# Four edits to a two-layer, four-way attention kernel: a scan operand, a one-column multiply, half of a subtraction and a scaling step change their place

## The chip, the cores and the metric

The kernel runs on one core of one Trainium2 chip. A core has TensorE (PE in the profile, its weight loads PEld), VectorE (DVE), ScalarE (ACT), GpSimd (POOL) and a queue engine (SP) that issues the transfers; they share the on-chip memory SBUF, and TensorE writes into PSUM, where this kernel has eight tiles of 128 partitions by 512 float32. The metric is the device time of one execution in microseconds (us), as the median of some runs.

## The reference

Two layers over a sequence of 2048 tokens, width 1024. Each layer projects the tokens, runs four groups of four heads (head size 64), gates, projects back and normalises:

- fox: causal softmax attention with a forget term; mla: causal softmax attention with low-rank projections and rotary parts; mem: softmax attention over 256 memory rows;
- sb, "stick-breaking": with z the scaled logits, the weight of key k for query q is `sigmoid(z[q,k])` times the product of `sigmoid(-z[q,k'])` over all valid keys k' behind k (k < k' < q). In the reference this product is the exponential of a reverse cumulative sum of `log_sigmoid(-z)`.

```
z = einsum('bhqd,bhkd->bhqk', qb, k) * scale
log_keep = where(valid, log_sigmoid(-z), 0)
log_tail = cumsum(log_keep, reverse) - log_keep
w = where(valid, exp(log_sigmoid(z) + log_tail), 0)
```

All is float32; the kernel carries each matrix operand as a float16 high part and a float16 low part.

## The kernel before, in words

Each layer goes through a list of stages (PLAN): the latent projections, then two head pairs each of fox, mla, sb and mem, then the output projection with its layer norm. A pair's work runs in four chunks of 512 queries: project keys, queries and values and the gate, then for each of the two heads and for each group g of two query tiles (128 queries each, j = 0 and 1; tile i = 2g + j) the attention. Keys are taken in blocks b of up to 1024: query tile i has one block of (i+1)*128 columns, or for i of 8 and more two blocks, (i-7)*128 and 1024 columns.

What happens to one sb block (`stick_tile`, `half`): PE writes the scores of up to 512 keys each into PSUM tiles `ps` (one or two a block, out of four buffers that scores and gates share). ACT makes two sigmoids of each `ps` into SBUF, `keep` (L400) and `w` (L401). DVE runs a product scan backwards over `keep` in place (L403): its first input is `keep`, its second operand is not used (op1 is bypass) and is `keep` again; it starts from `cy`, which is a constant for the last keys and for the other block the running product, copied out by L408. POOL multiplies the last column of `w` by `cy` (L404) and the other columns of `w` by the scanned `keep`, shifted by one (L405). ACT casts `w` to float16 (`hi`, L411), DVE subtracts that from `w` to the float16 low half (`lo`, L412), and SP issues the transposing transfer of both halves (L354), whose result PE multiplies with the values (L859). The tiles `hi`/`lo` have three buffers.

What happens to the softmax kinds (`softmax_tiles`, fox and mla): DVE copies the scores from PSUM to SBUF with a row maximum (L369 with the forget term, L371 without), reduces the maxima of both query tiles (L376) and scales them (L377, one instruction of 128x2); ACT takes the exponentials in place (L381), casts to `hi` (L388), POOL subtracts to `lo` (L389).

Each engine works through its own queue in order. The order of the queues is not written by hand: a planner lays the instructions out along its own estimate of the timeline, by the order in the program and by what is ready, so that instructions of neighbouring blocks and of the next chunk's projections stand between those of one block.

Of the kernel before, what the change touches and what calls it, by code (L numbers as in the profile page):

```python
# [13 lines left out]
AF = mybir.ActivationFunctionType  # L14
ALU = mybir.AluOpType
# [6 lines left out]
P = 128  # L22
# [18 lines left out]
LN_TOP = 15.0 * math.log(2.0)  # L41
# [8 lines left out]
def hybrid_kernel(ctx: ExitStack, tc: tile.TileContext, x, mem, ln_in_g, ln_in_b, mem_ln_g, mem_ln_b,  # L50
# [7 lines left out]
    def pool(name, bufs, space=None):  # L58
        if space is None:
            return ctx.enter_context(tc.tile_pool(name=name, bufs=bufs))  # L60
        return ctx.enter_context(tc.tile_pool(name=name, bufs=bufs, space=space))
# [13 lines left out]
    op = pool("op", 1)  # L75
# [8 lines left out]
    V, A, G, T = nc.vector, nc.scalar, nc.gpsimd, nc.tensor  # L84
# [4 lines left out]
    def nm(s):  # L89
        uid[0] += 1  # L90
        return f"{s}_{uid[0]}"
# [135 lines left out]
    def granule(name, shape=(P, 1024), dt=F32):  # L227
        return sbp.tile(list(shape), dt, name=nm(name), tag="sb")
# [89 lines left out]
    def scores(kind, h, i, b, qs, ks, qr, kr):  # L318

        n = min(1024, (i + 1) * P - 1024 * b)  # L320
        j = i % 4
        npass = 3 if kind == "mla" else 2
        parts = []
        with tc.high_priority(offset=SCORE_AHEAD.get(kind, 0)):
            for o in range(0, n, 512):
                c, m = 2 * b + o // 512, min(512, n - o)
                ps = s_tile()
                diag = c == i // 4
                for v in range(npass):
                    last = v == npass - 1 and not diag  # L330
                    if v < 2:
                        T.matmul(ps[:, :m], qs[:, h, v, j * P:(j + 1) * P], ks[c][:, h, :m], start=(v == 0), stop=last)  # L332
                    else:
                        T.matmul(ps[:, :m], qr[:, h, j * P:(j + 1) * P], kr[:, c * 4:c * 4 + m // P, :], start=False, stop=last)
                if diag:
                    T.matmul(ps[:, m - P:m], id_bf, masks["s" if kind == "sb" else "c"], start=False, stop=True)
                parts.append((ps, o, m))
        return parts, n
# [9 lines left out]
    def hl_tile(n):  # L348

        t = phl.tile([P, 2048], F16, name=nm("hl"), tag="phl")  # L350
        return t[:, :n], t[:, n:2 * n], t[:, :2 * n]

    def emit_T(both, n, pt, j):
        dmaT(pt[:, 16 * j:16 * j + 2 * (n // P), :], both)  # L354

    def softmax_tiles(kind, h, g, qs, ks, qr, kr, fb, sc, nsc, su):

        sm = smp.tile([P, 2, 8], F32, name=nm("sm"), tag="sm", bufs=8)
        nb = g // 4 + 1
        at, n_ = [[], []], [0, 0]  # L360
        for j in range(2):
            for b in range(nb):
                parts, n = scores(kind, h, 2 * g + j, b, qs, ks, qr, kr)
                t = granule("sb")[:, :n]
                for ps, o, m in parts:
                    mx = sm[:, j, 4 + n_[j]:5 + n_[j]]
                    n_[j] += 1
                    if kind == "fox":
                        V.tensor_tensor_reduce(t[:, o:o + m], ps[:, :m], fb[b][:, o:o + m], 1.0, -3.0e38, ALU.add, ALU.max, mx)  # L369
                    else:  # L370
                        V.tensor_scalar(t[:, o:o + m], ps[:, :m], 1.0, None, op0=ALU.mult, op1=ALU.max, accum_out=mx)  # L371
                at[j].append(t)
        top = sm[:, :, 4:5]
        if n_[0] > 1:
            top = sm[:, :, 0:1]
            V.tensor_reduce(top, sm[:, :, 4:4 + n_[0]], axis=AX.X, op=ALU.max)  # L376
        V.tensor_scalar(sm[:, :, 2:3], top, nsc, LN_TOP, op0=ALU.mult, op1=ALU.add)  # L377
        col = h * 4 + 2 * (g % 2)
        for j in range(2):
            for b, t in enumerate(at[j]):  # L380
                A.activation(t, t, AF.Exp, scale=sc, bias=sm[:, j, 2:3], accum_out=su[:, b, col + j:col + j + 1])  # L381

        def half(b, pt):
            for j in range(2):
                t = at[j][b]
                n = min(1024, (2 * g + j + 1) * P - 1024 * b)
                hi, lo, both = hl_tile(n)
                A.copy(hi, t)  # L388
                G.tensor_tensor(lo, t, hi, op=ALU.subtract)  # L389
                emit_T(both, n, pt, j)  # L390
        return half

    def stick_tile(h, i, j, qs, ks, sc, nsc):
        carry = [None]

        def half(b, pt):
            parts, n = scores("sb", h, i, b, qs, ks, None, None)
            keep, w = granule("kp")[:, :n], granule("sg")[:, :n]
            for ps, o, m in parts:
                A.activation(keep[:, o:o + m], ps[:, :m], AF.Sigmoid, scale=nsc)  # L400
                A.activation(w[:, o:o + m], ps[:, :m], AF.Sigmoid, scale=sc)  # L401
            cy = TOP if carry[0] is None else carry[0]
            V.tensor_tensor_scan(keep[:, ::-1], keep[:, ::-1], keep[:, ::-1], cy, op0=ALU.mult, op1=ALU.bypass)  # L403
            G.tensor_scalar(w[:, n - 1:n], w[:, n - 1:n], cy, 1.0, op0=ALU.mult, op1=ALU.mult)  # L404
            G.tensor_tensor(w[:, :n - 1], w[:, :n - 1], keep[:, 1:n], op=ALU.mult)  # L405
            if b:
                ct = smp.tile([P, 8], F32, name=nm("cy"), tag="cy", bufs=8)
                V.tensor_copy(ct[:, 0:1], keep[:, 0:1])  # L408
                carry[0] = ct[:, 0:1]
            hi, lo, both = hl_tile(n)  # L410
            A.copy(hi, w)  # L411
            V.tensor_tensor(lo, w, hi, op=ALU.subtract)  # L412
            emit_T(both, n, pt, j)
        return half

# [49 lines left out]
    def layer(l, hT, s_h, u_h, ah):  # L465
# [241 lines left out]
        def pair(kind, p):  # L707
# [54 lines left out]
            for c in range(NCH):  # L762
# [32 lines left out]
                for h in range(2):  # L795
# [34 lines left out]
                    for g in (2 * c, 2 * c + 1):  # L830
                        nb = (2 * g + 1) // 8 + 1
                        halves = []
                        if kind == "sb":
                            for j in range(2):
                                halves.append(stick_tile(h, 2 * g + j, j, qs, ks, sc, nsc))
                        else:
                            halves.append(softmax_tiles(kind, h, g, qs, ks, qr, kr, fb, sc, nsc, su))
# [235 lines left out]
```

## Time and profile before

| | |
|---|---|
| median of 3 runs | 3155.57 us (3152.43 to 3160.11) |
| the profiled execution's own time | 3160.48 us |
| its span | 3158.5 us |
| PE busy | 2557.1 us (81%) |
| DVE busy | 2280.7 us (72%) |
| ACT busy | 1913.3 us (61%) |
| POOL busy | 1561.7 us (49%) |
| mean granted TensorE clock | 0.91 |

The span runs from the first to the last instruction. Busy time is the time in which an engine has at least one instruction running; an instruction that has begun and is held up inside counts as busy. Matmuls overlap, so PE's busy time is more than what its array needs. The profile gives a chain of work that ended last, groups of instructions by source line, what ended each idle time, a timeline, and sums over any stretch. The two sb stages of layer 0 lie at some 870 to 1300 us, those of layer 1 at some 2400 to 2840 us; the fox and mla stages lie ahead of them, from some 250 and 1770 us.

### The profile page before, as it was taken

How to read it: one execution, taken by the hardware profiler on the slowest of the kernel's cores; microseconds unless marked ns; L12 is line 12 of the kernel's file. 1: busy time of each engine (PE TensorE's matmuls, PEld its weight loads, DVE VectorE, ACT ScalarE, POOL GpSimd, SP SyncE). 2: the span in 40 equal slices, each digit the busy share in tenths (PEclk: the TensorE clock that was granted, in tenths of full speed). 3: DMA queues.
4: the chain of work that ended last, by engine and by line, in shares of the span. 5: the costliest groups of instructions: out<-in, count | busy, mean ns of one | idle time of the engine just before them, and what ended most of it. 6: DMA issues, size and time to landing. Idle time of an engine off the chain costs nothing. (4 is left out here: it accounts for less than half of the span.)

```text
span 3158.5 us, 47091 instructions
## 1 busy us (share of the span) xinstructions
PE 2557.1 (81%) x16412; PEld 1374.9 (44%) x16412; DVE 2280.7 (72%) x4377; ACT 1913.3 (61%) x3543; POOL 1561.7 (49%) x1079
## 2 busy tenths in 40 slices
PE   2589897888986784798978899878889768659898
PEld 2345453444553442444434545444445435334443
DVE  7756767867679989757655475577676998994565
ACT  3447667877766676474234566677767766755600
POOL 5305545555678687443210246455657867772400
PEclk9889998999998897799989999999989889769999
DMA  7748978888755745657845478897977475465752
GB/s 190 196 126 167 191 154 188 176 174 174 150 103 115 155 87 112 139 119 191 235 116 126 90 162 163 165 189 157 176 157 135 91 168 101 96 148 114 170 181 100
DMA packets 1225038, 469.46 MB, mean 149 GB/s; under 512 B 1040304, under 2 KB 1184944, under 8 KB 1224656
## 3 DMA queue, kind: packets, MB, share of 16 engines
q1 hardware_dynamic: 1224800, 466.46, 67.8%
q8 instruction: 128, 2.10, 0.3%
q14 instruction: 110, 0.90, 0.1%
HBM read 141.07 MB, written 50.53 MB: 61 GB/s over the span
## 5 line engine op out<-in xcount | busy, mean ns | idle before, releaser
L389 POOL TENSOR_TENSOR hl<-sb,hl 128x1024 f16<-128x1024 f32 (+7 forms) x384 | 609.1, 1599 | 686.3 <-ACT hl L388 503.9
L332 PE MATMUL s<-k,q 128*128 128x512 f16 (+3 forms) x1920 | 529.4, 378 | 117.7 <-ACT sg L401 34.0
L859 PE MATMUL o<-pt,v 128*128 128x256 f16 (+3 forms) x3456 | 429.4, 299 | 200.3 <-DMA pt<-hl 194.8
L405 POOL TENSOR_TENSOR sg<-sg,kp 128x127 f32<-128x127 f32 (+3 forms) x192 | 384.4, 2004 | 119.7 <-DVE kp L403 95.3
L381 ACT ACTIVATE sb<-sb,sm,sc_all 128x1024 f32<-128x1024 f32 (+7 forms) x384 | 376.5, 981 | 76.0 <-DVE sm L377 75.4
L859 PEld LDWEIGHTS <-v 128*64 128x64 f16 (+1 forms) x3456 | 245.0, 112 | 401.7 <-DMA pt<-hl 201.3
L388 ACT CAST hl<-sb 128x1024 f16<-128x1024 f32 (+7 forms) x384 | 297.7, 791 | 184.2 <-DMA pt<-hl 174.0
L937 PE MATMUL s<-wo,gc 128*128 128x512 f16 x1536 | 335.2, 381 | 0.4 <-DVE yt L941 0.4
L332 PEld LDWEIGHTS <-q 128*128 128x128 f16 x1920 | 185.2, 104 | 321.0 <-issue 201.8
L412 DVE TENSOR_TENSOR hl<-sg,hl 128x128 f16<-128x128 f32 (+3 forms) x192 | 241.9, 1267 | 44.0 <-ACT hl L411 43.0
L411 ACT CAST hl<-sg 128x128 f16<-128x128 f32 (+3 forms) x192 | 152.9, 798 | 177.5 <-DMA pt<-hl 104.4
L369 DVE CUSTOM_DVE_ANT_0 sb<-s,fb 128x512 f32<-128x512 f32 (+2 forms) x320 | 184.3, 607 | 102.9 <-DMA fb<-fds 39.6
L371 DVE TENSOR_SCALAR_CACHE_REDUCE sb<-s 128x512 f32<-128x512 f32 (+2 forms) x320 | 185.5, 606 | 72.1 <-POOL hl L389 39.8
L937 PEld LDWEIGHTS <-gc 128*128 128x128 f16 x1536 | 150.9, 98 | 182.2 <-issue 3.9
L401 ACT ACTIVATE sg<-s,sc_all 128x512 f32<-128x512 f32 (+2 forms) x320 | 199.6, 629 | 40.4 <-POOL sg L405 22.1
L403 DVE TENSOR_TENSOR_SCAN kp<-kp 128x384 f32<-128x384 f32 (+7 forms) x128 | 216.6, 1705 | 8.8 <-ACT kp L400 7.7
L400 ACT ACTIVATE kp<-s,sc_all 128x512 f32<-128x512 f32 (+2 forms) x320 | 200.0, 627 | 29.0 <-PE s L332 9.4
L276 PE MATMUL pv<-w,hT 128*128 128x128 f16 x1024 | 191.6, 227 | 24.6 <-DVE k L286 24.6
L456 POOL TENSOR_TENSOR og<-og,sg 128x512 f32<-128x512 f32 x64 | 99.2, 1550 | 223.2 <-DVE og L452 124.0
L276 PE MATMUL pg<-hT,w 128*128 128x512 f16 x512 | 197.0, 385 | 8.1 <-DVE sb L371 3.7
L277 PE MATMUL pg<-hT,w 128*128 128x512 f16 x512 | 196.3, 383 | 0.0
L278 PE MATMUL pg<-hT,w 128*128 128x512 f16 x512 | 195.9, 383 | 0.0
(238 smaller groups left out, 5930.1 us busy)
## 6 DMA issues: line engine op xcount, KB each, us to landing
raw<-in_w_in_dram SPq DMA_DIRECT2D x100, 256.0 KB, 4.7
q<-q SPq DMA_DIRECT2D x128, 128.0 KB, 2.8
fb<-fds SPq DMA_DIRECT2D x32, 512.0 KB, 4.0
gd<-gh SPq DMA_DIRECT2D x128, 128.0 KB, 2.6
raw<-in_w_out_dram SPq DMA_DIRECT2D x64, 256.0 KB, 3.8
gc<-gd SPq DMA_DIRECT2D x64, 256.0 KB, 4.0
yt<-ah SPq DMA_DIRECT2D x32, 512.0 KB, 5.3
raw<-ctd SPq DMA_DIRECT2D x48, 256.0 KB, 3.1
```

The costliest lines, as they stand in the source:

```text
L276: T.matmul(ps, lh, rh, start=(first and k == 0), stop=False)
L332: T.matmul(ps[:, :m], qs[:, h, v, j * P:(j + 1) * P], ks[c][:, h, :m], start=(v == 0), stop=last)
L381: A.activation(t, t, AF.Exp, scale=sc, bias=sm[:, j, 2:3], accum_out=su[:, b, col + j:col + j + 1])
L388: A.copy(hi, t)
L389: G.tensor_tensor(lo, t, hi, op=ALU.subtract)
L400: A.activation(keep[:, o:o + m], ps[:, :m], AF.Sigmoid, scale=nsc)
L401: A.activation(w[:, o:o + m], ps[:, :m], AF.Sigmoid, scale=sc)
L403: V.tensor_tensor_scan(keep[:, ::-1], keep[:, ::-1], keep[:, ::-1], cy, op0=ALU.mult, op1=ALU.bypass)
L405: G.tensor_tensor(w[:, :n - 1], w[:, :n - 1], keep[:, 1:n], op=ALU.mult)
L412: V.tensor_tensor(lo, w, hi, op=ALU.subtract)
L859: T.matmul(o[r0:r1, oc + j0 * P:oc + 256], vs[k // 4][:, k % 4, h, 0:r1 - r0], pcol(pt, a, k % 8, kb, j0), start=(n == 1), stop=(n == total))
L937: T.matmul(ps, gc[a][k // 4][:, k % 4, t * P:(t + 1) * P], wo[k][:, b2, n * 512:(n + 1) * 512], start=(k == 0 and a == 0 and b2 == 0), sto ...
```

## The change

Four edits. The row numbers are those of the kernel before.

- L377: the scaling of the two maxima becomes two instructions of 128x1, one for each query tile.
- L403: the scan's unused second operand is no longer `keep` in SBUF but one column of the block's last score tile `ps` in PSUM, read again and again (stride 0).
- L404: the multiply of the last column of `w` by `cy` goes from GpSimd to ScalarE, as a copy with a scale.
- L412: the subtraction that makes the low half goes to GpSimd for the second query tile of each pair (j = 1); for j = 0 it stays on VectorE.

```diff
-        V.tensor_scalar(sm[:, :, 2:3], top, nsc, LN_TOP, op0=ALU.mult, op1=ALU.add)
+        for j in range(2):
+            V.tensor_scalar(sm[:, j, 2:3], top[:, j], nsc, LN_TOP, op0=ALU.mult, op1=ALU.add)
...
-            V.tensor_tensor_scan(keep[:, ::-1], keep[:, ::-1], keep[:, ::-1], cy, op0=ALU.mult, op1=ALU.bypass)
-            G.tensor_scalar(w[:, n - 1:n], w[:, n - 1:n], cy, 1.0, op0=ALU.mult, op1=ALU.mult)
+
+            V.tensor_tensor_scan(keep[:, ::-1], keep[:, ::-1], ps[:, 0:1].broadcast_to([P, n]), cy, op0=ALU.mult,
+                                 op1=ALU.bypass)
+            A.activation(w[:, n - 1:n], w[:, n - 1:n], AF.Copy, scale=cy)
...
-            V.tensor_tensor(lo, w, hi, op=ALU.subtract)
+            (G if j else V).tensor_tensor(lo, w, hi, op=ALU.subtract)
```

## Rows read from the trace of the kernel before

**Rows 1.** The page, part 1: busy us (share of the span) and instructions of each engine.

```profile
PE 2557.1 (81%) x16412; PEld 1374.9 (44%) x16412; DVE 2280.7 (72%) x4377; ACT 1913.3 (61%) x3543; POOL 1561.7 (49%) x1079
```

**Rows 2.** Sums over stretches: sb stages (first two rows), fox and mla of layer 0.

```profile
870.00:1300.00 430.00, 304.21 (x2091) 167.91 (x2090) 395.73 (x399) 284.03 (x495) 325.86 (x212) 0.84 0.59 117
...
sum 870.00, PE 625.55 PEld 348.44 DVE 800.39 ACT 580.84 POOL 659.32; mean PE 312.78 PEld 174.22 DVE 400.19 ACT 290.42 POOL 329.66
...
250.00:870.00 620.00, 531.29 (x3677) 292.57 (x3675) 436.69 (x1131) 451.79 (x791) 340.92 (x238) 0.94 0.85 173
```

**Rows 3.** Who waited for whom, 870 to 1300 us: total us, times, longest us.

```profile
POOL sg L405 <- DVE kp L403: 46.8, 19, 5.3
...
PE s L332 <- ACT sg L401: 17.4, 13, 6.1
```

**Rows 4.** Timeline, 2549 to 2558 us: start us, us, engine line operation.

```profile
2549.79 8.25 POOL L404 TENSOR_SCALAR sg<-sg,cy 128x1 f32<-128x1 f32 x1
...
2550.33 1.94 DVE L412 TENSOR_TENSOR hl<-sg,hl 128x1024 f16<-128x1024 f32 x2
...
2555.77 2.27 DVE L403 TENSOR_TENSOR_SCAN kp<-kp 128x1024 f32<-128x1024 f32 x1
...
2557.99 1.99 POOL L405 TENSOR_TENSOR sg<-sg,kp 128x1023 f32<-128x1023 f32 x1
```

**Rows 5.** Timeline, 466 to 471 us, POOL and then DVE.

```profile
466.33 4.61 POOL L389 TENSOR_TENSOR hl<-sb,hl 128x1024 f16<-128x1024 f32 x3 [0.89 <-ACT hl L388]
...
467.01 1.48 DVE L377 TENSOR_SCALAR sm<-sm,sc_all 128x2 f32<-128x2 f32 x1
...
469.24 0.69 DVE L369 CUSTOM_DVE_ANT_0 sb<-s,fb 128x512 f32<-128x512 f32 x1
```

**Rows 6.** Sums over both sb stretches of lines 403, 412, 404 and 405 alone.

```profile
sum 870.00, DVE 367.16; mean DVE 183.58
...
sum 870.00, DVE 237.26; mean DVE 118.63
...
sum 870.00, POOL 194.06; mean POOL 97.03
...
sum 870.00, POOL 380.23; mean POOL 190.12
```

**Rows 7.** Lines 403, 412 and 405, whole run: duration ns min/median/max.

```profile
L403 DVE TENSOR_TENSOR_SCAN kp<-kp x128: 399/1504/3787, 861.6 to 2819.9; 128x128 f32<-128x128 f32 x16, 128x256 f32<-128x256 f32 x16, 128x384 f32<-128x384 f32 x16, 128x512 f32<-128x512 f32 x16
L403 DVE TENSOR_TENSOR_SCAN kp<-kp,cy x64: 2320/2345/3478, 936.4 to 2829.7; 128x1024 f32<-128x1024 f32 x64
...
L412 DVE TENSOR_TENSOR hl<-sg,hl x192: 279/1202/3044, 875.1 to 2841.4; 128x1024 f16<-128x1024 f32 x80, 128x128 f16<-128x128 f32 x16, 128x256 f16<-128x256 f32 x16, 128x384 f16<-128x384 f32 x16
...
L405 POOL TENSOR_TENSOR sg<-sg,kp x192: 403/1990/6728, 862.1 to 2833.2; 128x1023 f32<-128x1023 f32 x80, 128x127 f32<-128x127 f32 x16, 128x255 f32<-128x255 f32 x16, 128x383 f32<-128x383 f32 x16
```

**Rows 8.** Groups by shape, whole run: count, busy us, mean ns, idle before, its releasers.

```profile
L389 POOL TENSOR_TENSOR hl<-sb,hl 128x1024 f16<-128x1024 f32 x160 | 344.5, 2163 | 186.1 <-ACT hl L388 166.8 <-DVE sb L371 5.8 <-DVE qr L656 4.5
...
L389 POOL TENSOR_TENSOR hl<-sb,hl 128x256 f16<-128x256 f32 x32 | 23.6, 738 | 61.8 <-ACT hl L388 61.8
```

**Rows 9.** Groups by shape, ACT, 870 to 1300 us.

```profile
L411 ACT CAST hl<-sg 128x1024 f16<-128x1024 f32 x39 | 40.8, 1047 | 50.2 <-DMA pt<-hl 27.1 <-POOL sg L405 23.1
...
L401 ACT ACTIVATE sg<-s,sc_all 128x128 f32<-128x128 f32 x14 | 5.2, 375 | 0.0
...
L411 ACT CAST hl<-sg 128x128 f16<-128x128 f32 x8 | 2.4, 295 | 1.2 <-DMA pt<-hl 1.1
```

**Rows 10.** Line 377 by shape; lines 485 and 445 by duration; who waited for 377.

```profile
L377 DVE TENSOR_SCALAR sm<-sm,sc_all 128x2 f32<-128x2 f32 x128 | 85.9, 674 | 2.7
...
L485 DVE TENSOR_SCALAR sc_all<-sc_all x46: 175/203/215, 68.8 to 2856.1; 128x1 f32<-128x1 f32 x46
...
L445 DVE TENSOR_TENSOR sg<-sg,rb x48: 664/686/690, 255.7 to 3014.3; 128x512 f32<-128x512 f32 x48
...
  ACT sb L381: 75.4, 47
```

## The prediction, made before the change was run

> **What bounds the kernel now.** I read the page's shares first: PE 81%, DVE 72%, ACT 61%, POOL 49% [rows 1]. No engine bounds the whole run, so I cut the span into stages. In the two sb stretches (870 us together) DVE is busy for 800.4 us, 92%, while PE has 625.6, ACT 580.8 and POOL 659.3 us; in the fox and mla stretch PE leads with 531.3 of 620 us, 86%, and the transfers have 85% [rows 2]. Three of the four edits lie in the sb stretches, and these are a matter of DVE.
>
> But DVE's busy time there is not all work. The timeline shows a GpSimd multiply of one column that lasts 8.25 us, from 2549.79 to 2558.04: just as long as DVE runs subtractions of two SBUF inputs (L412) and scans with two SBUF inputs (L403), almost back to back, and it ends when the last scan does; the POOL multiply behind it (L405) then takes 1.99 us [rows 4]. Elsewhere three POOL subtractions take 4.61 us, of which two have 1024 columns, while DVE runs L369, whose second input lies in PSUM, at its 0.69 us: neither delays the other; but the little L377, 128x2 in SBUF, needs 1.48 us there [rows 5]. So a DVE operation with two SBUF inputs and a GpSimd operation exclude each other, the one that comes later stands inside its busy time, and one with a PSUM input is free of it.
>
> [...]
>
> **How much is exclusion.** Lines through the shortest forms give the time without it. Scan: 399 ns at 128 columns, 2320 at 1024 [rows 7], that is 2.144 ns a column and 125 ns; 192 scans over 139,264 columns (8 heads of 17,408) make 322.5 us against 367.2 measured [rows 6], 44.7 us of waiting. L405: 403 ns at 127, 1990 (the median, also the bare case of [rows 4]) at 1023, so 1.771 ns and 178 ns: 281 us against 380.2. L412: 279 ns at 128 and its median, 1202, for 1024 columns: 1.03 ns and 147 ns, 172 us against 237.3. [...]
>
> **The change part by part** (both layers together).
>
> *Scan operand.* [...] Its own speed: no row shows a scan with a PSUM operand. The nearest is L445, one SBUF and one PSUM input, 512 columns in 686 ns [rows 10], against 147 + 512 x 1.03 = 674 for the two SBUF inputs of L412: 12 ns more, 192 times, 2 us. Bounds: 2.1 ns a column say that the scan is held by its recurrence, so 0 below; 26 ns (L445's whole spread, 664 to 690), 5 us, above. I take 0. [...]
> The scan now also waits for PE's scores, but ACT's sigmoids, for which it waited already, come behind these. The last `ps` of a block is freed by the scan's end and not by L401: PE waits, and behind it stand, in order, value matmuls of earlier blocks and projections. The price is a rival below; in the sum 0, since four buffers hold two blocks and the wait for L401 is small, 17.4 us in 430 [rows 3].
>
> *One column to ScalarE.* POOL loses 194.1 us [rows 6], nearly all of it waiting. ACT gains 192 instructions. L411 has 1047 ns at 1024 columns and 295 at 128, 0.84 ns a column, so 0.19 us at one column; L401 with its scale from SBUF 375 - 107 = 0.27 [rows 9]. 128 x 0.19 + 64 x 0.27 = 42 us (bounds 0, if all fall into ACT's idle third, and 128 x 0.295 + 64 x 0.375 = 62). On 64 of them ACT waits for the carry (L408), with casts and sigmoids queued behind; that carry is from the tile's block before, with the other tile's block between, so I take no stall.
>
> *Low halves of j = 1 to GpSimd.* j = 1 has 96 of 192 instructions and 9216 of 17,408 columns a head, 53%: 126 us leave DVE. On POOL L389 does the same operation: 2163 ns at 1024, 738 at 256 [rows 8], so 1.855 ns and 263 ns; 96 instructions, 73,728 columns: 162 us. POOL waits for ACT's cast with the next block's L405 queued behind it: for L389 that costs 166.8 / 160 = 1.04 us at 1024 columns and 1.93 at 256 [rows 8]; 0 to 185 us, I take 100. POOL then needs 659.3 - 194.1 - 380.2 + 281 = 366 for the rest, 528 with the low halves, 628 with the waits.
>
> *Scaling per tile.* 128 instructions of 674 ns become 256. A 128x1 scaling on DVE never takes over 215 ns (L485, median 203) [rows 10], whatever GpSimd does, so two take 0.41 us at most: 34 us off DVE. ACT waits 75.4 us for L377 [rows 10], but in that stretch PE and the transfers stand at 85% [rows 2], and DVE at 70%. Gain 0 to 34 us; I take 10.
>
> **The sum.** In the sb stretches DVE needs 800.4 - 44.7 - 126 = 630 us, PE 626, ACT 581 + 42 = 623, POOL 628. Four engines in one chain, each with the same load; how full can they be? DVE now reaches 92%, PE in the fox and mla stretch 86%. I take the lower, since now no one engine can run ahead: 630 / 0.86 = 733, so 137 us less. With 10 from the softmax stages: 147. The profiled execution took 3160.5 us (span 3158.5 and 2 around it); 3013. The median of the runs shown is 4.9 us lower: 3009.
>
> **The rivals.**
> - *Fuller.* DVE's 92% hold afterwards too, PE's clock rises from its granted 0.84 [rows 2] with fewer gaps, and all 34 us of L377 count: 630 / 0.92 = 685, 185 + 34 = 219 less: 2937. For it: a wait inside a queue also goes. Against: three more engines at 90%.
> - *PE held by the score buffers.* Each wait of PE for L401 (13 in the first stretch, about 26 in both) becomes a wait for a scan, 2.33 us longer: 61 us back, 86 gained: 3070. For it: PE does run into these buffers today. Against: DVE then lags ACT less. If ACT's and POOL's new waits add up to as much again: 3130, still faster.
> [...]
> - *Nothing moves*: the planner's new order of the queues, which I cannot read off, eats what the edits free, for instance by low halves placed ahead of a ready L405. Within 0.2% of before.
>
> **How the numbers follow.** Forecast 0.63, fuller 0.10, held by PE 0.18, port kept 0.05, nothing 0.04. The forecast's own range is 2960 to 3060 (fill 0.82 to 0.90, the unknown costs above); the range for 8 in 10 reaches to the fuller case and past the held one: 2935 to 3110. 0.2% (6 us) is about what a measurement of this kernel can tell from no change. Faster: 0.63 + 0.10 + 0.18, less 0.01 for a held PE that gives all back: 0.90. Within: 0.04. Slower: 0.06.
>
> **What would show it.** Scans at 2.32 to 2.35 us with little spread above; POOL's L405 near 1.99 us at 1023 columns though scans run beside it; the 128x1 steps of the softmax under 0.22 us; sb stretches of about 365 us each, with DVE at 310 to 320 us. Wrong: scans or L405 still stretched (port kept), PE's waits for the scan above 60 us in both stretches (held), or POOL idle behind ACT's cast above 180 us.

## The result: 2.9% faster, three fifths of the forecast gain

The changed kernel takes 3067.73 us (median of four runs, 3066.03 to 3069.9) against 3157.84 us for the kernel before: a ratio of 0.9714, 95% interval 0.97 to 0.9729. The forecast was 3009 us, so 90 us were gained where 147 were expected; the time lies inside the range of 2935 to 3110.

In the changed kernel five lines have new numbers: the scan is L405, the one-column multiply L407, the full multiply L408, the low half's subtraction L415; the scaling of the maxima is L378. The first row below is the page's first part of the changed kernel (busy us, share of the span, instructions), beside [rows 1].

```profile
PE 2528.2 (83%) x16412; PEld 1357.7 (44%) x16412; DVE 2098.1 (68%) x4409; ACT 1929.9 (63%) x3735; POOL 1436.6 (47%) x983
```

DVE lost 182.6 us of busy time and POOL 125.1, ACT gained 16.6. The next view sums both sb stretches, here cut from the start of a layer's first scan to the end of its last, to within 2 us; the columns are the stretch, its length, then busy us and instructions of PE, PEld, DVE, ACT and POOL, the granted clock, the transfers' share and GB/s. The third stretch is fox and mla of layer 0.

```profile
859.00:1246.00 387.00, 300.87 (x2114) 165.84 (x2113) 331.38 (x356) 299.65 (x602) 260.43 (x170) 0.86 0.64 128
2343.00:2736.00 393.00, 300.64 (x2143) 165.25 (x2142) 327.99 (x359) 302.38 (x606) 266.89 (x171) 0.87 0.65 130
sum 780.00, PE 601.51 PEld 331.10 DVE 659.37 ACT 602.03 POOL 527.32; mean PE 300.76 PEld 165.55 DVE 329.69 ACT 301.02 POOL 263.66
...
250.00:859.00 609.00, 522.47 (x3631) 287.34 (x3628) 411.59 (x1187) 443.16 (x781) 336.11 (x229) 0.95 0.87 175
```

The same cut of the kernel before (861 to 1296 and 2401 to 2834 us):

```profile
sum 868.00, PE 624.22 PEld 346.27 DVE 798.20 ACT 584.94 POOL 660.86; mean PE 312.11 PEld 173.14 DVE 399.10 ACT 292.47 POOL 330.43
```

So the sb stretches are 88 us shorter, where the forecast said 137; DVE is busy in them for 659 us (84.5%), where it said 630 us (86%). The fox and mla stretches of both layers, from the first row maximum of a layer (L369) to the end of its last (L371), went from 1237 to 1224 us, 13 against the forecast 10, and the rest of the kernel is some 6 us longer: 94 us of span.

Line by line the edits did what the forecast said of them. Sums over the two sb stretches, of L405, L407, L408 and L415 in this order:

```profile
sum 780.00, DVE 320.04; mean DVE 160.02
...
sum 780.00, ACT 46.16; mean ACT 23.08
...
sum 780.00, POOL 304.14; mean POOL 152.07
...
sum 780.00, DVE 129.35 POOL 161.49; mean DVE 64.68 POOL 80.74
```

And their durations over the whole run (ns min/median/max, first and last start, shapes), beside [rows 7, 10]:

```profile
L405 DVE TENSOR_TENSOR_SCAN kp<-kp,cy,s x64: 2311/2337/2349, 926.0 to 2732.3; 128x1024 f32<-128x1024 f32 x64
...
L407 ACT ACTIVATE sg<-sg x128: 188/203/286, 860.0 to 2730.2; 128x1 f32<-128x1 f32 x128
L407 ACT ACTIVATE sg<-sg,cy x64: 280/300/403, 927.4 to 2734.3; 128x1 f32<-128x1 f32 x64
...
L378 DVE TENSOR_SCALAR sm<-sm,sc_all x256: 192/206/216, 238.9 to 2332.8; 128x1 f32<-128x1 f32 x128
```

The scans went from 2320/2345/3478 to 2311/2337/2349: the second operand in PSUM neither slows the scan nor lets GpSimd hold it up. One row of the timeline (start us, duration us) from each of the two engines shows them at full speed beside each other:

```profile
1050.52 2.35 DVE L405 TENSOR_TENSOR_SCAN kp<-kp,cy,s 128x1024 f32<-128x1024 f32 x1 [0.82 <-ACT sg L402]
...
1051.49 2.13 POOL L415 TENSOR_TENSOR hl<-sg,hl 128x1024 f16<-128x1024 f32 x1 [0.36 <-ACT hl L414]
```

GpSimd's multiply beside them, the forecast's other sign, is near its bare 1.99 us too, though not always. By shape over the whole run (count, busy us, mean ns, idle before), the kernel before and then the changed one:

```profile
L405 POOL TENSOR_TENSOR sg<-sg,kp 128x1023 f32<-128x1023 f32 x80 | 210.5, 2632 | 77.2 <-DVE kp L403 62.4 <-DVE wt L170 11.8 <-ACT kp L400 2.4
```

```profile
L408 POOL TENSOR_TENSOR sg<-sg,kp 128x1023 f32<-128x1023 f32 x80 | 170.3, 2129 | 133.3 <-DVE kp L405 100.5 <-DVE wt L170 13.9 <-DVE wt L125 11.4
```

What is left of the exclusion shows in two other places. A VectorE subtraction with two SBUF inputs is now slower than before: by shape, 868 to 1250 us, 1778 ns at 1024 columns where bare it takes 1202 [rows 7]; over the whole run the mean of this shape is 1718 ns, against 1578 before. That GpSimd's own subtraction, 2116 ns in the median, makes the longer waits fits this, but no run separates it.

```profile
L415 DVE TENSOR_TENSOR hl<-sg,hl 128x1024 f16<-128x1024 f32 x15 | 26.7, 1778 | 1.9 <-ACT hl L414 1.8
L147 DVE SCALAR_TENSOR_TENSOR w<-raw,sc_all,w 128x512 f16<-128x512 f32 x18 | 25.2, 1446 | 0.0
```

And two small VectorE steps of the weight bounds (largest magnitudes, from which the weights' scales are made), which touch two columns, last 2 us each, as long as the GpSimd multiplies that began just before them (timeline):

```profile
2681.32 2.00 POOL L408 TENSOR_TENSOR sg<-sg,kp 128x1023 f32<-128x1023 f32 x1 [5.83 <-DVE wt L125]
2686.47 2.00 POOL L408 TENSOR_TENSOR sg<-sg,kp 128x1023 f32<-128x1023 f32 x1 [3.15 <-DVE kp L405]
...
2681.16 0.14 DVE L125 TENSOR_SCALAR wt<-wt 128x2 f32<-128x2 f32 x1
2681.34 2.00 DVE L135 TENSOR_SCALAR am<-wt 128x2 int32<-128x2 int32 x1
...
2686.54 1.95 DVE L141 TENSOR_SCALAR ad<-id_bf,at 2x2 bf16<-2x2 bf16 x1
```

A like step just ahead of the first multiply, L125 at 2681.16, takes 0.14 us. So two columns are held beside GpSimd here (2.00 and 1.95 us), and one column is not: L378 takes 216 ns at most in 256 cases, also while GpSimd subtracts (two of them 0.33 us together from 464.44, inside three L390 that run from 463.75 to 468.37). Why the second column makes the difference, no run shows.

Last, who waited for the scan. POOL does, as it must, since its multiply takes the scanned row (80.7 and 81.0 us in the two stretches). New is PE, for the score buffer that the scan now holds. The first row is of 868 to 1250 us, the second of 2341 to 2739 us (total us, times, longest us):

```profile
PE s L332 <- DVE kp L405: 37.1, 22, 8.5
...
PE s L332 <- DVE kp L405: 33.5, 25, 4.3
```

That is 71 us, over the 60 us in both stretches that the forecast had named as the sign of its rival "PE held by the score buffers", and that rival's time, 3070 us, is nearly the measured one. So the first question for the experiments was whether the missing 57 us are that wait.

### The profile page after: what moved, and what is told of

Same layout as the page of the kernel before. It is cut to its first block, busy times and chain, and to the rows that moved or that the text cites. A ratio compares the mean times of both kernels' runs of the same rounds, so it can differ in the third digit from the quotient of the medians.

```text
span 3064.1 us, 47280 instructions
## 1 busy us (share of the span) xinstructions
PE 2528.2 (83%) x16412; PEld 1357.7 (44%) x16412; DVE 2098.1 (68%) x4409; ACT 1929.9 (63%) x3735; POOL 1436.6 (47%) x983
## 5 line engine op out<-in xcount | busy, mean ns | idle before, releaser
L390 POOL TENSOR_TENSOR hl<-sb,hl 128x1024 f16<-128x1024 f32 (+7 forms) x384 | 606.8, 1592 | 696.8 <-ACT hl L389 530.8
L332 PE MATMUL s<-k,q 128*128 128x512 f16 (+3 forms) x1920 | 522.4, 373 | 184.1 <-DVE kp L405 71.0
L862 PE MATMUL o<-pt,v 128*128 128x256 f16 (+3 forms) x3456 | 411.9, 290 | 120.0 <-DMA pt<-hl 119.2
L408 POOL TENSOR_TENSOR sg<-sg,kp 128x127 f32<-128x127 f32 (+3 forms) x192 | 308.2, 1611 | 208.6 <-DVE kp L405 164.6
L862 PEld LDWEIGHTS <-v 128*64 128x64 f16 (+1 forms) x3456 | 238.3, 109 | 314.6 <-issue 138.5
L369 DVE CUSTOM_DVE_ANT_0 sb<-s,fb 128x512 f32<-128x512 f32 (+2 forms) x320 | 183.4, 605 | 99.4 <-DMA fb<-fds 43.2
L371 DVE TENSOR_SCALAR_CACHE_REDUCE sb<-s 128x512 f32<-128x512 f32 (+2 forms) x320 | 185.6, 605 | 81.4 <-POOL hl L390 38.1
L276 PE MATMUL pg<-hT,w 128*128 128x512 f16 x512 | 198.5, 388 | 10.6 <-DVE sb L371 10.5
L276 PEld LDWEIGHTS <-w 128*128 128x128 f16 x1264 | 126.6, 100 | 155.7 <-issue 11.7
L277 PEld LDWEIGHTS <-w 128*128 128x128 f16 x1264 | 126.6, 100 | 153.6 <-issue 31.9
L405 DVE TENSOR_TENSOR_SCAN kp<-kp,s 128x384 f32<-128x384 f32 (+7 forms) x128 | 171.4, 1344 | 31.2 <-ACT sg L402 27.7
```

The lines of the kernel that those rows point to most:

```text
L276: T.matmul(ps, lh, rh, start=(first and k == 0), stop=False)
L277: T.matmul(ps, lh, rl, start=False, stop=False)
L405: V.tensor_tensor_scan(keep[:, ::-1], keep[:, ::-1], ps[:, 0:1].broadcast_to([P, n]), cy, op0=ALU.mult, op1=ALU.bypass)
L862: T.matmul(o[r0:r1, oc + j0 * P:oc + 256], vs[k // 4][:, k % 4, h, 0:r1 - r0], pcol(pt, a, k % 8, kb, j0), start=(n == 1), stop=(n == total))
```

## The experiments

Ratios are to the kernel before, run on the same chip. Each edit is to the changed kernel unless said otherwise.

**Are the held score buffers the cause?** The plainest test takes the scan's operand from a PSUM tile that nobody else uses. The eight PSUM buffers are all taken, so the first three runs take one from the projections: p1 is that alone, p1_bank gives it to the scan's operand, p1_s5 to a fifth score buffer.

```diff
-    ps_p = pool("ps_p", 2, bass.MemoryType.PSUM)
+    ps_p = pool("ps_p", 1, bass.MemoryType.PSUM)          # p1, p1_bank, p1_s5
+    ps_c = pool("ps_c", 1, bass.MemoryType.PSUM)          # p1_bank
+    pc = ps_c.tile([P, 512], F32, name="pc")
+    V.memset(pc[:, 0:1], 1.0)
-    ... tensor_tensor_scan(..., ps[:, 0:1].broadcast_to([P, n]), cy, ...
+    ... tensor_tensor_scan(..., pc[:, 0:1].broadcast_to([P, n]), cy, ...
-    ps_s = pool("ps_s", 4, bass.MemoryType.PSUM)
+    ps_s = pool("ps_s", 5, bass.MemoryType.PSUM)          # p1_s5
```

> The changed kernel with one PSUM buffer instead of two for the projections, and one PSUM tile left unused: the control for the next two. Both theories: slower than the changed kernel (3067 us) by the waits of the projections for their one buffer, 0 to 80 us; PE's waits for the scan about as in the changed kernel, 81 us (71 at the matmul, 10 at its weight load).

> As the control, but the scan's unused operand is one column of a PSUM tile of its own, written once at the start, so that the scan holds no score buffer. Theory A (the gain that is missing, some 55 us, is PE waiting for score buffers that the scan holds): 40 to 70 us under the control, PE's waits for the scan gone, the scans still at 2.3 us. Theory B (those waits of PE are slack, and the chain of DVE, POOL and ACT sets the sb stages): within 15 us of the control, other waits in their place.

> As the control, with the spare PSUM tile given to the scores, five buffers instead of four, the scan's operand in the block's last score tile as in the change. Theory A: 20 to 50 us under the control, PE's waits for the scan at most half. Theory B: within 15 us of the control.

Measured: p1 3324.14 us (1.0525, 1.051 to 1.0541), p1_bank 3320.76 us (1.0522, 1.0499 to 1.0544), p1_s5 3324.83 us (1.0527, 1.0511 to 1.0544). One projection buffer costs 256 us against the changed kernel, far more than expected, and stretches the sb stages too (432 + 433 us). Between the three there is no difference, although PE's wait for the scan is 110.6 us in p1 and 121.6 in p1_s5, and in p1_bank PE's wait for a score buffer has another releaser, the second sigmoid (numbered L405 there):

```profile
PE s L335 <- ACT sg L405: 54.2, 57, 6.7
```

This tells that the wait is worth nothing where the projections set the pace; of the changed kernel, where they don't, it tells little.

**first**: the operand comes from the block's first score tile instead of its last.

```diff
-    ... ps[:, 0:1].broadcast_to([P, n])
+    ... parts[0][0][:, 0:1].broadcast_to([P, n])
```

> The changed kernel, but the scan's unused operand is a column of the block's first score tile instead of its last. Blocks of over 512 columns (128 of 192) hold the buffer that PE needs first. Theory A: PE's waits for the scan grow from 81 us to 100 to 150, and the time by 15 to 50 us over the changed kernel's 3067. Theory B: within 15 us of 3067.

Measured: 3062.09 us (0.9697, 0.9681 to 0.9712), PE's wait for the scan 70.7 us in 46 pieces, as before the edit. Which of a block's two buffers is held matters little; the theory by which PE's waits grow to 100 us and more when the earlier one is held falls.

**s3 and s3_bank**: here the buffer comes from the scores themselves. s3 has three score buffers and the operand in `ps`; s3_bank has three and the operand in a tile of its own, so the only difference between the two is whether the scan holds a score buffer, under more pressure than with four.

```diff
-    ps_s = pool("ps_s", 4, bass.MemoryType.PSUM)
+    ps_s = pool("ps_s", 3, bass.MemoryType.PSUM)          # s3, s3_bank; s3_bank also with pc as in p1_bank
```

> The changed kernel with three score buffers instead of four, one PSUM tile unused; the scan holds one. Control for the next. Theory A (PE's wait for buffers that the scan holds is the missing gain): the sb stretches, 779 us together in the change, grow by over 80 us. Theory B (these waits are slack): by 0 to 40 us. Both: the fox and mla stretches lose some time too.

> As the control with three score buffers, with the spare PSUM tile as the scan's own operand: no score buffer is held. Theory A: sb stretches at or below the change's 779 us, 50 us or more under the control. Theory B: within 25 us of the control. Fox and mla stretches as in the control.

Measured: s3 3132.32 us (0.991, 0.9886 to 0.9935), s3_bank 3123.07 us (0.9881, 0.9854 to 0.9908): 9 us apart, the intervals overlapping; the sb stretches sum to 800 and 782 us. The waits of PE over the whole run, s3 and then s3_bank (L335, L865 and L405 there are the score matmul, the value matmul and the second sigmoid):

```profile
PE o L862 <- DMA pt<-hl: 127.8, 97, 6.9
PE s L332 <- DVE kp L405: 100.7, 48, 10.6
```

```profile
PE o L865 <- DMA pt<-hl: 192.6, 112, 7.1
PE s L335 <- ACT sg L405: 43.0, 39, 4.5
```

100 us of waiting for the scan are gone and some 9 us of time with them (18 in the sb stretches). Most of the wait has only moved: the value matmuls wait 65 us more for the transposed halves, and the score matmuls 43.0 us for the second sigmoid, where s3 has 10.5. With four buffers the wait for the scan is shorter. So PE's 71 us are slack for the most part: PE waits there, or it would wait for the next thing a little later. The rival's price of 61 us is not what happened; that its sum met the measured time is chance.

**no_scan**: the scan's operand back in SBUF, the other edits kept.

```diff
-            V.tensor_tensor_scan(keep[:, ::-1], keep[:, ::-1], ps[:, 0:1].broadcast_to([P, n]), cy, op0=ALU.mult,
-                                 op1=ALU.bypass)
+            V.tensor_tensor_scan(keep[:, ::-1], keep[:, ::-1], keep[:, ::-1], cy, op0=ALU.mult, op1=ALU.bypass)
```

> The changed kernel with the scan's unused operand back in SBUF (the other three edits stay). Theory P (in the sb stages the exclusion of DVE's two-input operations and POOL is the bound, and the scan's operand is what lifts it): scans, both multiplies' main part and the low halves exclude each other again, 847 us by my lines, so 3140 to 3185 us, with scans and POOL's L408 stretched. Theory Q (DVE's own load is the bound, and the gain is from the low halves taken off it): only the scans' 45 us of waiting come back, 3100 to 3120 us.

Measured: 3183.55 us (1.0081, 1.0063 to 1.01), 116 us above the changed kernel and slower than before. The scan's row, and both sb stretches:

```profile
L404 DVE TENSOR_TENSOR_SCAN kp<-kp,cy x64: 2321/2450/4204, 931.8 to 2846.1; 128x1024 f32<-128x1024 f32 x64
...
sum 885.00, PE 620.39 PEld 344.54 DVE 781.85 ACT 602.49 POOL 676.26; mean PE 310.20 PEld 172.27 DVE 390.92 ACT 301.24 POOL 338.13
```

Scans of up to 4.2 us are back, POOL rises by 149 us and DVE by 122. Of the 116 us, 105 lie in the sb stretches, and they come back though this scan holds no score buffer. So the scan edit carries the change: the other three without it lose 0.8%. That is theory P, at the upper end of its 3140 to 3185 us. Its 847 us are the forecast's lines added up: 322.5 for the scans, 281 for the full multiply, 162 for the low halves on GpSimd and 82 for those left on VectorE (96 x 147 ns + 65,536 x 1.03 ns). That no two of these steps run beside each other is the author's estimate, and the closeness is partly luck: counted from scan to scan the sb stretches take 883 us, 17 longer than before (866), fox and mla are 10 shorter, and the rest of the kernel is 19 longer.

**no_lo**: all low halves on VectorE.

```diff
-            (G if j else V).tensor_tensor(lo, w, hi, op=ALU.subtract)
+            V.tensor_tensor(lo, w, hi, op=ALU.subtract)
```

> The changed kernel with all low halves of the sb stages back on VectorE. Theory P: the pair is not the bound without the scan, so this gives back only what DVE's load asks: 655 + 110 us in 780, 3100 to 3130 us. Theory Q: all of the sb stages' gain goes, 3145 to 3160 us.

Measured: 3101.24 us (0.9825, 0.9811 to 0.9839), so the low halves on GpSimd are worth 34 us, as theory P had it (3100 to 3130 us; its pair is that of VectorE's two-input steps and GpSimd). With all of them on VectorE, DVE works 727.16 of 810 us, 90%:

```profile
sum 810.00, PE 605.82 PEld 336.95 DVE 727.16 ACT 602.53 POOL 388.61; mean PE 302.91 PEld 168.48 DVE 363.58 ACT 301.27 POOL 194.30
```

Moving 96 subtractions took 68 us off DVE (727 to 659), not 126: L415's own time on DVE fell by 99 (228.0 to 129.4), and other steps lengthened, L147 from 35.8 to 48.7.

**no_col**: the one-column multiply back on GpSimd.

```diff
-            A.activation(w[:, n - 1:n], w[:, n - 1:n], AF.Copy, scale=cy)
+            G.tensor_scalar(w[:, n - 1:n], w[:, n - 1:n], cy, 1.0, op0=ALU.mult, op1=ALU.mult)
```

> The changed kernel with the one-column multiply back on GpSimd. Theory P: its 1 us was waiting behind scans; without them it takes 0.2 to 0.5 us and costs at most 15 us, 3065 to 3080 us. Theory Q, or POOL's queue as the bound: its 194 us come back on POOL, 3100 us or more.

Measured: 3040.03 us (0.9628, 0.9611 to 0.9645): 27 us *faster* than the changed kernel. Both expectations missed. The multiply's rows and the sb stretches:

```profile
L407 POOL TENSOR_SCALAR sg<-sg x128: 180/190/1027, 863.1 to 2707.2; 128x1 f32<-128x1 f32 x128
L407 POOL TENSOR_SCALAR sg<-sg,cy x64: 254/264/1317, 930.4 to 2714.6; 128x1 f32<-128x1 f32 x64
...
sum 754.00, PE 592.84 PEld 329.19 DVE 647.27 ACT 570.31 POOL 557.92; mean PE 296.42 PEld 164.59 DVE 323.64 ACT 285.16 POOL 278.96
```

Once the scan has its second operand in PSUM, the step that took 194 us on POOL before [rows 6] costs 0.19 and 0.26 us a piece, 41 us in all by their medians and 57 as measured in the two stretches (some are still held, up to 1.3 us), and POOL has room. On ACT it costs 46 us of the engine that also makes both sigmoids and the cast of every block. PE's wait for the scan is 86.1 us in this run over the whole trace, 15 *more* than in the changed kernel, and the run is faster: a second witness that this wait does not set the time. What does fall is the wait of the value matmuls for the transposed halves: in the sb windows of 868 to 1250 and 2341 to 2739 us of the changed kernel, and of 868 to 1240 and 2333 to 2712 us of no_col:

```profile
PE o L862 <- DMA pt<-hl: 21.8, 13, 5.0
...
PE o L862 <- DMA pt<-hl: 18.2, 13, 3.7
```

```profile
PE o L862 <- DMA pt<-hl: 15.7, 10, 3.1
...
PE o L862 <- DMA pt<-hl: 8.1, 6, 2.6
```

The waits of both subtractions for ACT's cast fall in the same windows, from 55.7 to 39.1 us. That fits an ACT that reaches its casts earlier. It is a reading, not a proof: the order of the queues changed too.

**soft_only**: the kernel before, with the scaling per tile alone.

```diff
-        V.tensor_scalar(sm[:, :, 2:3], top, nsc, LN_TOP, op0=ALU.mult, op1=ALU.add)
+        for j in range(2):
+            V.tensor_scalar(sm[:, j, 2:3], top[:, j], nsc, LN_TOP, op0=ALU.mult, op1=ALU.add)
```

> The kernel before with the softmax scaling per query tile alone. Both theories: DVE 34 to 45 us less busy in the fox and mla stages, 5 to 15 us gained there, nothing in the sb stages: ratio 0.995 to 0.9985. If those stages were bound by DVE: 0.988. If by PE and the transfers alone: 1.000.

Measured: 3169.74 us (1.0041, 1.0029 to 1.0054), slower than before, against the expectation. The fox and mla stretches are 11 us shorter (1226 against 1237 us), as forecast; but the sb stretches, in which nothing was edited, sum to 882 us from scan to scan, 16 more. The planner orders the whole program again after any edit: in the first sb stretch VectorE's order differs from the fourth instruction on. So a difference of some 15 us between two versions can't be put down to the edit between them; and as this is one case, 15 us is no bound either.

**scan_lo**: the reverse, the scan and the low halves without the one-column step and without the scaling per tile.

```diff
-            A.activation(w[:, n - 1:n], w[:, n - 1:n], AF.Copy, scale=cy)
+            G.tensor_scalar(w[:, n - 1:n], w[:, n - 1:n], cy, 1.0, op0=ALU.mult, op1=ALU.mult)
...
-        for j in range(2):
-            V.tensor_scalar(sm[:, j, 2:3], top[:, j], nsc, LN_TOP, op0=ALU.mult, op1=ALU.add)
+        V.tensor_scalar(sm[:, :, 2:3], top, nsc, LN_TOP, op0=ALU.mult, op1=ALU.add)
```

> The kernel before with two of the edits, the scan's operand and the low halves: the one-column multiply stays on GpSimd and the scaling of both tiles in one instruction. Against the run with three edits (3040 us, the multiply on GpSimd). If the scaling per tile gains in the fox and mla stages what its shorter waits say, and moves nothing else: 3046 to 3055 us. If what it cost alone (3170 against 3156) is its own: 3024 to 3030. If that was a new order of the queues by chance: anything within 15 us of 3040.

Measured: 3050.89 us (0.9662, 0.9638 to 0.9686), 11 us above no_col, where the forecast had 10 for the scaling; by soft_only, that is about the size of what the planner alone can do. It is also 17 us below the changed kernel, with sb stretches of 757 against 778 us from scan to scan: a second run without the one-column step on ScalarE that is faster there, though it lacks the scaling per tile too.

**ones**: no_col, and the two-column VectorE scalings of the weight bounds issued column by column, as the change does with L377 (lines 121, 125, 135 and 141; the first stands for all).

```diff
-        V.tensor_scalar(u, u, 0.5, None, op0=ALU.mult)
+        for i in range(n):
+            V.tensor_scalar(u[:, i:i + 1], u[:, i:i + 1], 0.5, None, op0=ALU.mult)
```

> As the run with three edits (3040 us), and the small VectorE scalings of two columns in the bounds of the weights (lines 121, 125, 135 and 141, some 18 us of busy time in each sb stretch before, nearly all of it waiting for POOL) are issued one column at a time. Theory P: they no longer wait, 20 to 35 us less DVE busy time in the sb stretches, and where DVE is full this counts: 3015 to 3035 us. Theory A or any in which DVE is not what fills the stages: 3035 to 3050.

Measured: 3020.64 us (0.9558, 0.9533 to 0.9582), 19 us below no_col and 47 below the change: the fastest of all the kernels run here. One of the four lines in no_col (L135) and in ones (L138), then the sb stretches of ones:

```profile
L135 DVE TENSOR_SCALAR am<-wt x32: 134/170/2080, 30.6 to 2731.4; 128x2 int32<-128x2 int32 x26, 128x1 int32<-128x1 int32 x6
```

```profile
L138 DVE TENSOR_SCALAR am<-wt x58: 100/144/156, 30.7 to 2712.2; 128x1 int32<-128x1 int32 x58
...
sum 745.00, PE 587.90 PEld 325.37 DVE 616.76 ACT 572.45 POOL 569.54; mean PE 293.95 PEld 162.68 DVE 308.38 ACT 286.23 POOL 284.77
```

The longest goes from 2080 to 156 ns. In the sb stretches the four lines go from 38.3 to 10.2 us, and DVE from 647 to 617 us. The sb stretches give 9 of the 19 us, the fox and mla stretches 4; the rest lies outside both and is not traced to a place.

## Why the prediction held, and where it fell short

**What bounds the kernel** was read right. The exclusion between VectorE steps with two SBUF inputs and GpSimd was the load: putting only the scan back costs 116 us, 105 of them in the sb stretches. That the 847 us of steps taken to exclude each other gave a range that holds that kernel's 3183.55 us was partly luck.

**Scan operand.** Right. 320.0 us against 322.5, so the 44.7 us of waiting left it (367.2 before), and no loss of speed; of the three prices for a PSUM source (0, 2 and 5 us) the 0 was the right one, 2337 ns against 2345 at 1024 columns. That its recurrence holds the scan, the reason given for the 0, is the author's inference from 2.1 ns a column (L412 has 1.03); the runs show only that its pace does not hang on where the second operand lies. The case with a chance of 0.05, "port kept", in which the scan stays stretched beside GpSimd, did not come: the longest of the 64 scans that start from a carry took 2349 ns, against 3478 before.

**PE held by the score buffers**, 0 in the sum. The sign of it came (71 us of waits against the 60 named), the loss did not: 9 us of time with three buffers, not resolved from nothing, while PE's waits moved to the transposed halves and the second sigmoid. The sign was badly chosen; a wait counts only as far as the engine has nothing else that would stop it next.

**Low halves.** 161.5 us on POOL against 162. The wait for ACT's cast, taken as 100 us (0 to 185), is 23.8 us in the two stretches (8.2 and 15.6). The gain was 34 us.

**Scaling per tile.** At most 216 ns each against 215 (two of which are 0.43 us; the forecast's "0.41 at most" is by the median); 13 us of the softmax stretches against 10. This is not resolved from the planner's doing: of the kernels here with four score and two projection buffers, those with this edit take 1221 to 1234 us there, the two without it 1232 (scan_lo) and 1237.

**One column to ScalarE: the step that failed.** Its size was right, 46 us against 42. It was taken as lying beside other work, on an ACT with an idle third, and as relief for POOL. Both were judged against the kernel before. POOL's 194 us were nearly all waiting, as the prediction itself says, and behind scans: the first edit had already removed them, so this edit took 57 us off POOL, which had room, and added 46 to ACT, which then is as loaded as PE (602 us each). It costs 27 us, more than the 15 that the planner moved in soft_only. 26 of them lie in the sb stretches, which fell 49 us short (137 forecast, 88 measured). How much of the 27 is ACT's place in the chain, and how much another order, stays open.

**DVE's need, mis-sized.** 630 us forecast, 659 measured. The forecast took the average wait out with the instructions moved, and let L412's rest keep its old mean: 237 - 126 = 111 us. It is 129.4, and L147, which has two SBUF inputs too, rose from 40.0 to 48.7; that GpSimd's subtractions, 2116 ns in the median, hold these steps up fits this, but was not tested alone. 659 / 0.86 = 767 us, 34 of the missing us by the forecast's own rule. The two-column steps were in no term; issuing them by column takes 28 us off DVE in ones, and 19 off the whole.

**How full.** 86% of DVE was a choice; 84.5% came. Against those 767 us the stretches are 780: 13 us. (These 34 and 13 split the same shortfall by DVE's load; the one-column step's 26 us lie within it, not beside it.) In the changed kernel the stages are not evenly mixed, as three neighbouring pieces of one sb stretch show (columns as above):

```profile
925.00:1050.00 125.00, 95.61 (x633) 51.16 (x632) 120.08 (x135) 93.91 (x182) 79.22 (x48) 0.88 0.69 148
1050.00:1150.00 100.00, 89.97 (x740) 53.43 (x737) 81.11 (x84) 84.61 (x179) 69.17 (x52) 0.97 0.58 113
1150.00:1225.00 75.00, 40.82 (x176) 17.41 (x175) 69.02 (x82) 51.98 (x100) 45.43 (x26) 0.64 0.55 113
```

DVE is full (96%) while PE has 76%, then PE is full (90%) while DVE has 81%, then DVE again with PE at 54% and a granted clock of 0.64. By these busy shares the limit changes hands, which a bound from one engine's sum over the stage misses; that this accounts for the 13 us is a reading.

## What to carry to other kernels

A short instruction that stays busy for long can be a wait that no idle column shows; compare its shortest and longest case (here 8.25 us for one column [rows 4], against 0.25 at the shortest in no_col), and look at what the other engine runs at that moment. A VectorE operand that is read but not used can come from PSUM, and a two-column scaling can be issued as two of one column: here both stepped out of GpSimd's way (scans of 1024 columns 2349 ns at most, scalings 216). Price the edits of one change in the company of each other: an edit that removes a wait can make the one that moves the waiting instruction needless, and then only its cost is left.

## What the runs showed of the hardware

- A scan with one SBUF and one PSUM operand (read with stride 0) ran beside GpSimd undisturbed in the changed kernel, 2311 to 2349 ns for 1024 columns in 64 cases, and not slower than with two SBUF operands in the kernel before (2320 at the shortest, 3478 at the longest).
- One-source VectorE steps on 128x2 in SBUF last up to 2.17 us beside GpSimd (L377 in scan_lo, 0.21 us at the least); on 128x1 the longest of 256 took 216 ns (L378 in the changed kernel). Two such instructions took less time on average than one of two columns: 2 x 206 ns by the median against a mean of 674 [rows 10].
- By the medians a one-column GpSimd multiply in no_col was as cheap as ScalarE's copy in the changed kernel: 190 ns against 203, and 264 against 300 with a scale from SBUF. The longest took 1027 and 1317 ns, against 286 and 403.
